# Transposing expert activations in 32x32 blocks on VectorE, with matrix columns taken in strides

## Chip, core and metric

The kernel runs on one core of a Trainium2 chip. The metric is device time in microseconds, from the first to the last instruction and the little around them; the median of several runs counts. The engines are TensorE (PE, with its weight loads PEld), VectorE (DVE), ScalarE (ACT), GpSimd (POOL) and SyncE (SP). SyncE's queue issues the transfers of the expert weights.

## What is computed

One layer of a diffusion backbone over 512 latent and 256 context tokens: attention and Fourier mixing, then a mixture of 32 experts, four to a token. The change touches the experts only. For each expert `e`, with the rows `xb` of the tokens that chose it:

```
g = minimum(xb @ w_gate[e] + b_gate[e], 7)
u = clip(xb @ w_up[e] + b_up[e], -7, 7)
act = g * sigmoid(1.702 * g) * (u + 1)
y = act @ w_down[e] + b_down[e]          # times the token's gate, added to its row
```

All three matrices are 1024 x 1024 in float32, 4 MB each, so 403 MB of expert weights are read.

## The kernel before

The first part (up to about 340 us) is attention, projections and the router. The rest is the mixture stage, in which the change lies.

**Units.** Experts are sorted by how many tokens they have, and each is a unit of a kind: heavy ("h", 128 slots, 4 experts), medium ("m", 96 slots used, 13 experts with the two that are always units 0 and 1), light ("l", 64 slots, 10 experts), tiny ("t", 32 slots, 5 experts). What doesn't fit goes to a loop at the end. From unit 2 on, units come in pairs: a heavy or medium one with a light or tiny one. There are ten medium-light pairs, four heavy-tiny pairs, and the first pair is medium-tiny. Within a pair the matrices alternate (`order`, L951 to L956): "gate" of the first, "gate" of the second, then both "up", then both "down".

**Weights.** Each matrix comes in four pieces of 1 MB (`load_piece`, L963 to L978) into a ring of eleven slots. Each piece holds two chunks `k` of 128 rows, which lie on the 128 partitions. A piece is issued by SyncE as soon as TensorE has done with the piece that lies in its slot.

**Matmuls.** `emit_mat` (L1650) runs eight steps `k` per matrix. `step_mm` (L1538) uses TensorE in column tiles: for a medium expert, twelve matmuls per step, each 32 tokens wide with 256 weight columns as the moving operand, four of them side by side in four tiles of 32 columns; for a light one two matmuls, 64 tokens wide with 512 weight columns; for a tiny one four, 32 wide with 256 columns. A heavy expert uses 128 columns and float32r with split operands. The trace records each float32 matmul as two MATMULs. The sums lie in PSUM (`ps`) in such a way that the partition tells the tile (which quarter or half of the weight columns, and which token), and not the token alone. A bias row is added first by a bfloat16 matmul (`biasP`).

**Between the matrices.** `glu_g` (L1458) and `glu_u` (L1468) do the activation: VectorE takes the sums out of PSUM into `t1` and `u1` (for light and tiny units `aTf` and `u1l`), ScalarE computes the sigmoid. `a_trans` (L1441) then transposes the activations, 128x128 at a time, on TensorE (`tr`, L268, line L270 in the trace) into PSUM bank 6 or 7, from which ScalarE copies them to `aTm` or `aTf` (`split_late` for heavy experts). They are the stationary operand of the "down" matrix. `y_out` scales the result and `scatter` (L1512) adds it to the token rows by one-hot matmuls.

**Order.** Everything in this stage stands in an order written out by the program. Work between matrices is a list of side tasks; after each step of a matrix up to two of them advance (`side_step`). `glu_u` yields a few times (2, 2, 3 or 5 steps by kind) ahead of `a_trans`, so that the transposes stand some steps into the next matrix. TensorE, VectorE and ScalarE each take their instructions in that order.

Of the kernel before, what the change touches and what calls it, by code (L numbers as in the profile page):

```python
# [31 lines left out]
AF = mybir.ActivationFunctionType  # L32
# [4 lines left out]
D = 1024  # L37
# [125 lines left out]
def dit_block(ctx: ExitStack, tc: tile.TileContext, x, c, cctx, c_ctx, w_mod, b_mod, n_ap, n_ao, n_fp, n_fo,  # L163
# [76 lines left out]
    def later(fn, outs, ins, age=1):  # L240
        if not manual:
            fn()
            return
        late.append([age, [touched(z) for z in outs], [touched(z) for z in ins], fn])
# [23 lines left out]
    def tr(o, i):  # L268
        guard([o], [i])
        pin(nc.tensor.transpose(o, i, ident))  # L270

    def act(o, i, f, **kw):
        guard([o] + ([kw["accum_out"]] if "accum_out" in kw else []), [i, kw.get("bias"), kw.get("scale")])
        return nc.scalar.activation(o, i, f, **kw)  # L274
# [976 lines left out]
        nc.gpsimd.memset(z.f, 0.0)  # L1251

    SLOTS = {"h": 128, "m": 128, "l": 64, "t": 32}

    def onehot_slots(kind, p_):
        n = SLOTS[kind]
# [28 lines left out]
    def tbank():  # L1285
        tb[0] = (tb[0] + 1) % len(tbanks)
        return tbanks[tb[0]]
# [152 lines left out]

    def a_trans(kind):  # L1441
        a = glu_tiles(kind)[1]
        for half in range(2 if kind in "hm" else 1):
            b = tbank()
            n = min(4, WIDTH[kind] // 128 - 4 * half)
            for k in range(n):
                c = (4 * half + k) * 128
                tr(ps[:, b, k * 128:k * 128 + 128], a[:, c:c + 128])
            src = ps[:, b, 0:n * 128].rearrange("p (k n) -> p k n", k=n)
            c4 = slice(4 * half, 4 * half + 4)  # L1450
            if kind == "h":
                split_late(aTh.r[:, c4], aTl.r[:, c4], src)
            else:
                z = (aTm if kind == "m" else aTf.f)[:, 4 * half:4 * half + n]
                later(lambda src=src, z=z: act(z, src, AF.Copy), [z], [src], age=0)
            yield

    def glu_g(kind, b):  # L1458
        t_, u_ = glu_tiles(kind)
# [78 lines left out]
    def step_mm(kind, mat, b, k, w, hi, lo, sel, xs):  # L1538

        first = k == 0  # L1540
        if kind == "h":
            xh, xl = xs
            if first and mat != "d":
                for h in range(2):
                    mm(ps[:, b + h], sel.to_broadcast([96, 128]), biasP.b[0:96, MAT[mat], h * 512:h * 512 + 512],
                       start=True, stop=False)
                first = False
            for st, mv, last in ((xh, hi, False), (xh, lo, False), (xl, hi, k == 7)):
                for h in range(2):
                    mm(ps[:, b + h], st.r[:, k], mv.r[:, h * 512:h * 512 + 512], start=first, stop=last)  # L1550
                first = False
        elif kind == "m":

            def unit(r, p):
                return (p, r) if p < 3 else (r, 3)

            def out_(r, p, n=1):
                return ps[32 * p:32 * p + 32, b + r // 2, 256 * (r % 2):256 * (r % 2) + 256 * n]


            both = ps[96:128, b].rearrange("p (r n) -> p r n", r=2)
            if first:
                bias = biasP.b[0:96, MAT.get(mat, 0)]
                if mat != "d":
                    for p in range(3):
                        mm(out_(0, p, 2), sel.to_broadcast([96, 32]), bias[:, 0:512], start=True, stop=False)
                else:
                    sel = selb.b[0:96, NS + 2:NS + 3]
                mm(both, sel.to_broadcast([96, 32]), bias[:, None, 768:D].to_broadcast([96, 2, 256]), start=True,
                   stop=False)  # L1570
                if mat != "d":
                    for p in range(4):
                        q = unit(2, p)[1]
                        mm(out_(2, p), sel.to_broadcast([96, 32]), bias[:, q * 256:q * 256 + 256], start=True, stop=False)
            for r in range(3):
                for p in range(4):
                    g, q = unit(r, p)
                    n = 1
                    if mat != "d":
                        st = xs[:, k, 32 * g:32 * g + 32]  # L1580
                    else:
                        fq, c = k // 2, k % 2
                        st = xs[:, 2 * fq + c, 32 * g:32 * g + 32] if fq < 3 else xs[:, 2 * g + c, 96:128]
                        if first and p < 3 and r < 2:
                            if r:
                                continue
                            n = 2
                    mm(out_(r, p, n), st, w[:, q * 256:q * 256 + 256 * n],
                       start=first and mat == "d" and (p < 3 or r == 2), stop=k == 7 and r > 0)
        else:  # L1590
            v, n = (64, 512) if kind == "l" else (32, 256)
            a, c = k // (n // 128), k % (n // 128)
            st = xs[:, c, v * a:v * a + v]
            if first and mat != "d":
                for h in range(128 // v):
                    mm(ps[v * h:v * h + v, b, 0:n], sel.to_broadcast([96, v]),
                       biasP.b[0:96, MAT[mat], h * n:h * n + n], start=True, stop=False)
                first = False
            for h in range(128 // v):
                mm(ps[v * h:v * h + v, b, 0:n], st, w[:, h * n:h * n + n], start=first, stop=k == 7)  # L1600

    def sel_of(u):
        kind, e, r = units[u]
# [69 lines left out]
    for i, (u, m) in enumerate(order):  # L1673
        kind = kinds[u]
        if i:
            pu, was = order[i - 1]
            pk, pb = kinds[pu], bank[pu, was]
            if was == "g":
                add(glu_g(pk, pb), True)
            elif was == "u":  # L1680
                acted[pu] = add(chain(glu_u(pk, pb, {"h": 2, "m": 2, "l": 3, "t": 5}[kind]), a_trans(pk)), True)
            else:
                finish(summed)
                y_out(pu, pk, pb)
                if pu == 1:
                    summed = add(chain(chain_back(pu), scatter(pu)))
                elif pk in "lt":
                    summed = add(chain(chain_back(pu - 1), chain_back(pu), scatter(pu - 1, pu)))
        if i == 5:
            summed = add(chain(bdown(), chain_back(0), scatter(0)))  # L1690
        if i == 1:
            ready[1] = add(x_of(1))
        elif i == 2:
            add(fetch_of(2))
            add(fetch_of(0))
            add(fetch_of(3))
        elif i == 3:
            ready[2] = add(chain(x_of(2), fetch_of(4)))
            add(chunk_plan())
        elif i == 6:  # L1700
            ready[3] = add(chain(x_of(3), fetch_of(5)))
        elif m == "d" and u >= 2 and u + 2 < NU:
            x_ = x_of(u + 2)
            ready[u + 2] = add(chain(x_, fetch_of(u + 4)) if u + 4 < NU else x_)
        if (u, m) == (NU - 4, "g"):
            ntot, jcnt = W(1, dt=I32), W(1)
            cp(ntot.i, incl.f[:, NE - 1:NE])
            V.memset(jcnt.f, 0.0)
            n_over = nc.values_load(ntot.i[0:1, 0:1], min_val=0, max_val=48, skip_runtime_bounds_check_because=SKIP)
        if m == "g":  # L1710
            finish(ready.get(u))
        elif m == "d":
            finish(acted.get(u))
        if i + 1 == len(order):
            break
        emit_mat(i)
        if i == 0:
            settle()
            t1, u1 = W(D), W(D)
            xT1 = W(8, 128)  # L1720
        elif i == 1:
            while side:
                finish(side.pop(0))
            queued.close()
            free(lg, mask, maskb, Ub, onesb)
            aTh, aTl = R(8, 128), R(8, 128)
            aTm = alias(aTh, 6, 128)
            yh, yl = R(D), R(D)
            acc = [W(D) for _ in range(4)]

            bdr = acc[3]
            for r in range(3):
                nc.sync.dma_start(bdr.f[32 * r:32 * r + 32], b_d)
        elif i == 4:
            settle()
            free(xT1)
            bd, gT, g3 = R(D), R(512), W(4, 96)
            xTf = W(4, 128)
        elif i == 6:
            while side and side[0] is not ready[3]:  # L1740
                finish(side.pop(0))
            settle()
            free(bd, g3, gT)
            aTf, u1l, yz = W(4, 128), W(512), R(D)

    while side:
        finish(side.pop(0))
# [136 lines left out]
```

## Time and profile before

| | us |
|---|---|
| three runs | 1412.1, 1416.8, 1417.2 |
| median | 1416.8 |
| the profiled execution, its own time | 1413.2 |
| its span | 1411.4 |
| TensorE busy | 1345.5 |
| VectorE busy | 719.9 |
| ScalarE busy | 409.3 |
| stage from 360 to 1380: TensorE's granted clock | 1.00, but for one stretch |

[...] In rows in order of time, the first column is the start and the second how long the group was busy; a group ends where the next begins or a little after, since matmuls overlap. "128*32 128x256" is a stationary operand of 128 rows and 32 columns with a moving one of 128 rows and 256 columns. A row takes the shape of its first instruction, so that one that begins with a bias matmul (96 rows, bf16) may hold others. Matmul ends are modelled; starts are measured.

### The profile page before, as it was taken

To read this page: it belongs to the slowest core of one execution; us is meant where nothing else is said; L and a number is where in the kernel's file an instruction comes from. 1 tells how busy PE (TensorE), PEld (TensorE's weight loads), DVE (VectorE), ACT (ScalarE), POOL (GpSimd) and SP (SyncE) were. 2 spreads that over 40 slices of the span, in tenths; PEclk is the share of its full clock that TensorE was granted. 3 is DMA by queue.
4 is the path that set the end of the run, shared out by engine and by line. 5 is a ranking of instruction groups with operands and counts; after the bars stand their busy time and mean duration, and the time that the engine had idled before them with its cause. 6 is when DMAs were issued, how large, how long until landed. Compare 5 with 4: busy or idle time off the path is not lost. (4 is left out here: it accounts for less than half of the span.)

```text
span 1411.4 us, 30490 instructions
## 1 busy us (share of the span) xinstructions
PE 1345.5 (95%) x12966; PEld 798.2 (57%) x12967; DVE 719.9 (51%) x1329; ACT 409.3 (29%) x634; POOL 121.8 (9%) x90
## 2 busy tenths in 40 slices
PE   5998999998999999999999999999999999999993
PEld 3766887877554545466444454654544466444572
DVE  4676777755452424268423335762324287232575
ACT  5565455632110101035110103421111154010352
POOL 4355000013000000000000000000000000000002
PEclk8999999999998999999999999999999999999997
DMA  9865003667887999999999999999999999999993
GB/s 343 306 229 189 1 0 106 216 228 313 315 295 298 408 397 408 379 409 392 405 409 379 409 374 409 396 408 406 393 384 385 401 395 408 402 408 375 408 380 122
DMA packets 126496, 468.86 MB, mean 332 GB/s; under 512 B 10976, under 2 KB 12316, under 8 KB 126356
## 3 DMA queue, kind: packets, MB, share of 16 engines
q1 hardware_dynamic: 121540, 454.44, 83.2%
q0 software_dynamic: 4816, 12.43, 2.3%
q8 instruction: 103, 1.69, 0.5%
q14 instruction: 37, 0.30, 0.1%
HBM read 464.05 MB, written 6.31 MB: 333 GB/s over the span
## 5 line engine op out<-in xcount | busy, mean ns | idle before, releaser
L266 PE MATMUL ps<-s,s 128*32 128x256 f32 (+11 forms) x5364 | 892.4, 417 | 28.7 <-DMA s<-in_w_mod_dram 8.4
L266 PEld LDWEIGHTS ps<-s,s 128*128 128x128 f32 (+4 forms) x5033 | 510.8, 155 | 315.2 <-issue 182.2
L266 PE MATMUL ps<-s,a 128*32 128x256 f32 (+1 forms) x7026 | 412.7, 383 | 0.0
L266 PEld LDWEIGHTS ps<-s,a 128*32 128x32 f32 x7026 | 216.7, 110 | 158.5 <-issue 18.9
L274 ACT ACTIVATE s<-s 128x1024 fp32r<-128x1024 f32 (+8 forms) x196 | 175.9, 927 | 361.7 <-DVE s L283 308.4
L278 DVE TENSOR_TENSOR s<-s,s 128x1024 fp32r<-128x1024 f32 (+11 forms) x316 | 208.4, 686 | 32.3 <-ACT s L274 28.6
L274 ACT ACTIVATE s<-ps 128x512 fp32r<-128x512 f32 (+5 forms) x168 | 91.3, 553 | 246.0 <-PE ps L266 127.1
L278 DVE TENSOR_TENSOR s<-s,ps 128x512 f32<-128x512 f32 (+1 forms) x129 | 86.5, 682 | 82.1 <-PE ps L266 81.7
L285 DVE TENSOR_SCALAR s<-ps 128x768 f32<-128x768 f32 (+3 forms) x32 | 26.3, 823 | 185.1 <-PE ps L266 185.1
L270 PE MATMUL ps<-s,s 128*128 128x128 f32 x575 | 96.6, 288 | 15.3 <-DVE s L283 9.9
L1302 POOL DMA_INDIRECT s<-hx_d,s x31 | 32.4, 1045 | 893.3 <-PE ps L266 613.2
L270 PEld LDWEIGHTS ps<-s,s 128*128 128x128 f32 x575 | 66.4, 143 | 73.7 <-issue 45.8
L293 DVE COPY s<-ps 128x4 f32<-128x4 f32 (+5 forms) x66 | 23.7, 359 | 141.0 <-PE ps L266 117.0
L274 ACT ACTIVATE a<-ps 128x512 f32<-128x512 f32 (+1 forms) x48 | 25.9, 540 | 219.0 <-PE ps L270 219.0
L278 POOL TENSOR_TENSOR s<-s,s 128x1024 f32<-128x1024 f32 (+1 forms) x23 | 53.7, 2339 | 272.9 <-DVE s L278 211.4
L289 DVE SCALAR_TENSOR_TENSOR s<-ps,s,s 32x256 fp32r<-32x256 f32 (+5 forms) x64 | 46.2, 721 | 58.0 <-ACT s L274 52.0
L274 ACT ACTIVATE s<-ps,s 32x256 fp32r<-32x256 f32 (+7 forms) x68 | 44.8, 669 | 97.9 <-PE ps L266 90.5
L297 DVE TENSOR_TENSOR s<-ps,s 128x512 fp32r<-128x512 f32 (+1 forms) x92 | 60.6, 667 | 22.9 <-ACT s L274 22.8
L283 DVE TENSOR_SCALAR s<-ps 128x768 f32<-128x768 f32 (+4 forms) x33 | 26.5, 803 | 77.6 <-PE ps L266 77.5
L274 ACT ACTIVATE s<-s,s 128x1 f32<-128x1 f32 (+4 forms) x70 | 43.2, 644 | 13.8 <-DVE s L289 7.7
L297 DVE TENSOR_TENSOR s<-s,s 128x192 fp32r<-128x192 f32 (+5 forms) x32 | 36.0, 1144 | 8.5 <-ACT s L274 8.5
L289 DVE SCALAR_TENSOR_TENSOR s<-s,s,s 128x512 fp32r<-128x512 f32 (+5 forms) x48 | 36.8, 796 | 5.9 <-ACT s L274 4.6
(77 smaller groups left out, 289.4 us busy)
## 6 DMA issues: line engine op xcount, KB each, us to landing
s<-in_w_gate_dram SPq DMA_DIRECT2D x128, 1024.0 KB, 10.9
s<-in_w_up_dram SPq DMA_DIRECT2D x128, 1024.0 KB, 10.8
s<-in_w_down_dram SPq DMA_DIRECT2D x128, 1024.0 KB, 7.9
s<-in_w_mod_dram SPq DMA_DIRECT2D x32, 512.0 KB, 4.6
s<-in_w_mod_dram SPq DMA_DIRECT2D x8, 1024.0 KB, 16.3
s<-in_x_dram SPq DMA_DIRECT2D x8, 512.0 KB, 8.3
s<-in_w_out_dram SPq DMA_DIRECT2D x8, 512.0 KB, 5.1
s<-in_w_in_dram SPq DMA_DIRECT2D x1, 2560.0 KB
```

What stands on the lines that cost most here:

```text
L266: pin(nc.tensor.matmul(o, a, b, start=start, stop=stop))
L270: pin(nc.tensor.transpose(o, i, ident))
L274: return nc.scalar.activation(o, i, f, **kw)
L278: return eng.tensor_tensor(o, a, b, op=op)
L283: eng.tensor_scalar(o, a, s1, s2, op0=op0)
L285: eng.tensor_scalar(o, a, s1, s2, op0=op0, op1=op1)
L289: V.scalar_tensor_tensor(o, a, s, b, op0=op0, op1=op1)
L293: eng.tensor_copy(o, i)
L297: later(lambda: eng.tensor_tensor(lo, src, hi, op=OP.subtract), [lo], [src, hi])
L1302: nc.gpsimd.indirect_dma_start(out=xg[kind], out_offset=None, in_=src, in_offset=bass.IndirectOffsetOnAxis(ap=idxs.i[:, u:u + 1], axis=0), ...
```

## The change

Medium, light and tiny activations are no longer transposed by TensorE. VectorE does it, in blocks of 32x32: one instruction takes 128 partitions by eight blocks of 32 columns and turns each block over within its 32 partitions. A medium unit needs three such instructions, a light one two, a tiny one one. `glu_u` no longer yields ahead of them, so they stand right behind the activation. The heavy units keep their transposes.

For the result to be a full transpose, the sums of "gate" and "up" have to lie differently in PSUM: partition 32q + i must hold token i and those columns whose number modulo 128 lies in the q-th 32. So in these two matrices each column tile q now takes its 256 moving columns in eight runs of 32, 128 apart (`cols`), and the bias likewise. Medium and tiny units keep their number of matmuls; light ones go from two 64-wide of 512 columns to eight 32-wide of 256. The "down" matrix keeps its form for each kind and only reads the stationary operand from its new place (`aTm` and `aTf` have new shapes of the same size).

```diff
+    ROWS = {"h": 128, "m": 96, "l": 64, "t": 32}
...
     def a_trans(kind):
         a = glu_tiles(kind)[1]
-        for half in range(2 if kind in "hm" else 1):
-            b = tbank()
-            n = min(4, WIDTH[kind] // 128 - 4 * half)
-            for k in range(n):
-                c = (4 * half + k) * 128
-                tr(ps[:, b, k * 128:k * 128 + 128], a[:, c:c + 128])
-            src = ps[:, b, 0:n * 128].rearrange("p (k n) -> p k n", k=n)
-            c4 = slice(4 * half, 4 * half + 4)
-            if kind == "h":
+        if kind == "h":
+            for half in range(2):
...
                 split_late(aTh.r[:, c4], aTl.r[:, c4], src)
-            else:
-                z = (aTm if kind == "m" else aTf.f)[:, 4 * half:4 * half + n]
-                later(lambda src=src, z=z: act(z, src, AF.Copy), [z], [src], age=0)
-            yield
+                yield
+            return
+        for s in range(ROWS[kind] // 32):
+            o = (aTm if kind == "m" else aTf.f)[:, :, 32 * s:32 * s + 32]
+            i_ = a[:, 256 * s:256 * s + 256].rearrange("p (b r) -> p b r", r=32)
+            guard([o], [i_])
+            V.transpose(o, i_)
+        yield
...
+        elif mat != "d":
+
+            n = ROWS[kind] // 32
+
+            def x_cols(o):
+                m, v = {"m": (8, 0), "l": (4, 64), "t": (2, 32)}[kind]
+                return xs[:, k % m, v * (k // m) + o:v * (k // m) + o + 32]
+
+            def cols(z, q):
+                return z.rearrange("p (b q r) -> p q b r", q=4, r=32)[:, q]
+
+            def tile_(q, s, n=1):
+                return ps[32 * q:32 * q + 32, b + s // 2, 256 * (s % 2):256 * (s % 2) + 256 * n]
+
+            if first:
+                for s in range(0, n, 2):
+                    m = min(2, n - s)
+                    for q in range(4):
+                        z = cols(biasP.b[0:96, MAT[mat]], q)
+                        o = tile_(q, s, m)
+                        if m == 2:
+                            o = o.rearrange("p (m b r) -> p m b r", m=2, r=32)
+                            z = z[:, None].to_broadcast([96, 2, 8, 32])
+                        mm(o, sel.to_broadcast([96, 32]), z, start=True, stop=False)
+            for s in range(n):
+                for q in range(4):
+                    mm(tile_(q, s), x_cols(32 * s), cols(w, q), start=False,
+                       stop=k == 7 and (s % 2 == 1 or s + 1 == n))
...
-                acted[pu] = add(chain(glu_u(pk, pb, {"h": 2, "m": 2, "l": 3, "t": 5}[kind]), a_trans(pk)), True)
+                acted[pu] = add(chain(glu_u(pk, pb, {"h": 2, "m": 2, "l": 3, "t": 5}[kind] if pk == "h" else 0), a_trans(pk)), True)
...
-            aTm = alias(aTh, 6, 128)
+            aTm = alias(aTh, 8, 96)
...
-            aTf, u1l, yz = W(4, 128), W(512), R(D)
+            aTf, u1l, yz = W(8, 64), W(512), R(D)
```

What this does to the order of the instructions is seen best on TensorE in a light unit's "up" matrix (first medium-light pair). Here `s_67` is the identity, `s_2877` is `u1` with the medium unit's activations, `s_3463` (then `s_3458`) the light unit's tokens, and the other names are ring slots with weights. Before:

```order
L266 MATMUL ps<-s_2343,s_3463 64x512 x4
L266 MATMUL ps<-s_2537,s_3463 64x512 x4
L270 MATMUL ps<-s_67,s_2877 128x128 x4
L266 MATMUL ps<-s_2545,s_3463 64x512 x2
L270 MATMUL ps<-s_67,s_2877 128x128 x2
L266 MATMUL ps<-s_2545,s_3463 64x512 x2
L266 MATMUL ps<-s_2553,s_3463 64x512 x4
```

And now:

```order
L266 LDWEIGHTS s_2597
L266 MATMUL ps<-s_1972,s_2597 32x512
L266 MATMUL ps<-s_2343,s_3458 32x256 x16
L266 MATMUL ps<-s_2537,s_3458 32x256 x16
L266 MATMUL ps<-s_2545,s_3458 32x256 x16
L266 MATMUL ps<-s_2553,s_3458 32x256 x16
```

The two groups of transposes are gone, nothing stands in their places, and every 64x512 matmul has become four of 32x256.

On VectorE at the same place, from the medium unit's activation to the place table of a later unit (`s_2876` and `s_2877` are `t1` and `u1`, `s_3747` and `s_3748`, now `s_3737` and `s_3738`, are `aTf` and `u1l`). Before:

```order
L285 TENSOR_SCALAR s_2877<-ps 128x768
L289 SCALAR_TENSOR_TENSOR s_2877<-s_2877,s_2876 128x768
L285 TENSOR_SCALAR s_3748<-ps 128x512
L289 SCALAR_TENSOR_TENSOR s_3748<-s_3748,s_3747 128x512
L278 TENSOR_TENSOR s_2724<-s_2335,s_2732 128x128
```

And now (`a_3014` is `aTm`):

```order
L285 TENSOR_SCALAR s_2877<-ps 128x768
L289 SCALAR_TENSOR_TENSOR s_2877<-s_2877,s_2876 128x768
L1459 STREAM_TRANSPOSE a_3014<-s_2877 128x8x32 x3
L285 TENSOR_SCALAR s_3738<-ps 128x512
L289 SCALAR_TENSOR_TENSOR s_3738<-s_3738,s_3737 128x512
L1459 STREAM_TRANSPOSE s_3737<-s_3738 128x8x32 x2
L278 TENSOR_TENSOR s_2724<-s_2335,s_2732 128x128
```

Five instructions have come in, each group right behind the activation it transposes.

The third place is VectorE in a heavy "down" matrix, where it splits the heavy unit's weights into two parts (the 128x1024 rows) a few steps ahead of TensorE. Before:

```order
L285 TENSOR_SCALAR s_3748<-ps 128x256
L289 SCALAR_TENSOR_TENSOR s_3748<-s_3748,s_3747 128x256
L278 TENSOR_TENSOR s_2594<-s_2695,s_2593 128x1024
L278 TENSOR_TENSOR s_2588<-s_2708,s_2587 128x1024
L278 TENSOR_TENSOR s_2724<-s_2335,s_2732 128x128
```

And now:

```order
L285 TENSOR_SCALAR s_3738<-ps 128x256
L289 SCALAR_TENSOR_TENSOR s_3738<-s_3738,s_3737 128x256
L1459 STREAM_TRANSPOSE s_3737<-s_3738 128x8x32
L278 TENSOR_TENSOR s_2594<-s_2695,s_2593 128x1024
L278 TENSOR_TENSOR s_2588<-s_2708,s_2587 128x1024
L278 TENSOR_TENSOR s_2724<-s_2335,s_2732 128x128
```

One transpose has come in ahead of the splits. The orders of GpSimd and of SyncE have no new and no missing instruction.

## Rows read from the trace of the kernel before

**Rows 1.** Stretches: busy us by engine, clock granted, DMA share, rate.

```profile
core 0: us, PE busy (x) PEld busy (x) DVE busy (x) ACT busy (x) POOL busy (x), PEclk, DMA share, GB/s
...
600.00:800.00 200.00, 197.83 (x1993) 106.27 (x1995) 95.45 (x174) 48.45 (x67) 6.44 (x6) 1.00 1.01 400
...
433.60:447.20 13.60, 12.87 (x60) 6.20 (x64) 6.08 (x10) 0.00 (x0) 0.00 (x0) 0.50 0.51 194
```

**Rows 2.** Waits from 360 to 1380 us: total, times, longest.

```profile
...
PEld ps L266 <- DVE s L278: 20.4, 25, 2.2
PEld ps L266 <- DMA s<-in_w_up_dram: 2.9, 10, 0.4
...
SPq L978 <- PE ps L266: 672.7, 315, 8.4
```

**Rows 3.** DMA, 600 to 1380 us: rate by slice, total, an issue group.

```profile
GB/s 408 379 410 407 410 402 408 409 355 410 408 355 399 408 409 384 409 408 403 408 408 353 393 408 399 363 409 408 386 409 407 395 411 407 395 360 408 409 383 371
DMA packets 81003, 309.49 MB, mean 397 GB/s; under 512 B 5639, under 2 KB 5643, under 8 KB 80924
...
s<-in_w_up_dram SPq DMA_DIRECT2D x96, 1024.0 KB, 10.8
```

**Rows 4.** TensorE in order of time: a light "gate", then that expert's "up".

```profile
696.85 7.27 PE L266 MATMUL ps<-s,s 96*64 96x512 bf16 x34
...
714.85 3.84 PE L266 MATMUL ps<-s,s 96*64 96x512 bf16 x18
718.63 0.66 PE L270 MATMUL ps<-s,s 128*128 128x128 f32 x4
...
720.59 2.79 PE L266 MATMUL ps<-s,s 128*64 128x512 f32 x12
```

**Rows 5.** TensorE in order of time: a medium "up", then that expert's "down".

```profile
704.28 0.28 PE L266 MATMUL ps<-s,s 96*32 96x256 bf16 x4
...
704.39 10.54 PE L266 MATMUL ps<-s,a 128*32 128x256 f32 x192
...
723.32 1.68 PE L266 MATMUL ps<-s,a 128*32 128x512 f32 x18
724.93 0.66 PE L270 MATMUL ps<-s,s 128*128 128x128 f32 x4
725.52 1.50 PE L266 MATMUL ps<-s,a 128*32 128x256 f32 x24
726.95 0.66 PE L270 MATMUL ps<-s,s 128*128 128x128 f32 x4
```

**Rows 6.** TensorE in order of time: inside a heavy "down" matrix.

```profile
660.06 0.60 PE L270 MATMUL ps<-s,s 128*128 128x128 f32 x4
660.41 1.64 PE L266 MATMUL ps<-s,s 128*128 128x512 f32 x6
661.89 0.38 PE L270 MATMUL ps<-s,s 128*128 128x128 f32 x2
662.03 2.36 PE L266 MATMUL ps<-s,s 128*128 128x512 f32 x9
```

**Rows 7.** VectorE in order of time: under the same heavy "down" matrix.

```profile
659.58 0.41 DVE L285 TENSOR_SCALAR s<-ps 128x256 f32<-128x256 f32 x1
...
660.37 2.55 DVE L278 TENSOR_TENSOR s<-s,s 128x1024 fp32r<-128x1024 f32 x3
```

**Rows 8.** Groups by line and shape, 360 to 1400 us: busy us, mean ns.

```profile
L285 DVE TENSOR_SCALAR s<-ps 128x768 f32<-128x768 f32 x13 | 12.5, 958 | 107.8 <-PE ps L266 107.8
...
L285 DVE TENSOR_SCALAR s<-ps 128x256 f32<-128x256 f32 x5 | 2.1, 415 | 2.8 <-PE ps L266 2.8
...
L274 ACT ACTIVATE a<-ps 128x512 f32<-128x512 f32 x35 | 20.9, 598 | 208.5 <-PE ps L270 208.5
```

**Rows 9.** Matmuls of two short stretches: ns min/median/max; value projection first.

```profile
L266 PE MATMUL ps<-s,s x19: 277/281/287, 111.2 to 113.4; 128*128 128x256 f32 x19
...
L266 PE MATMUL ps<-s,s x12: 280/282/392, 147.6 to 149.0; 128*128 128x256 f32 x11, 128*128 128x512 f32 x1
```

More of the change, by code (lines that the diff above doesn't have):

```diff
@@ L1442, in a_trans @@
         a = glu_tiles(kind)[1]
-        for half in range(2 if kind in "hm" else 1):
-            b = tbank()
-            n = min(4, WIDTH[kind] // 128 - 4 * half)
-            for k in range(n):
-                c = (4 * half + k) * 128
-                tr(ps[:, b, k * 128:k * 128 + 128], a[:, c:c + 128])
-            src = ps[:, b, 0:n * 128].rearrange("p (k n) -> p k n", k=n)
-            c4 = slice(4 * half, 4 * half + 4)
-            if kind == "h":
-                split_late(aTh.r[:, c4], aTl.r[:, c4], src)
-            else:
-                z = (aTm if kind == "m" else aTf.f)[:, 4 * half:4 * half + n]
-                later(lambda src=src, z=z: act(z, src, AF.Copy), [z], [src], age=0)
-            yield
+        if kind == "h":
+            for half in range(2):
+                b = tbank()
+                for k in range(4):
+                    c = (4 * half + k) * 128
+                    tr(ps[:, b, k * 128:k * 128 + 128], a[:, c:c + 128])
+                src = ps[:, b].rearrange("p (k n) -> p k n", k=4)
+                c4 = slice(4 * half, 4 * half + 4)
+                split_late(aTh.r[:, c4], aTl.r[:, c4], src)
+                yield
[6 more added lines that the diff above has]
+        yield
     def glu_g(kind, b):
@@ L1558, in out_ @@
                 return ps[32 * p:32 * p + 32, b + r // 2, 256 * (r % 2):256 * (r % 2) + 256 * n]
-            both = ps[96:128, b].rearrange("p (r n) -> p r n", r=2)
             if first:
[L1563 to L1574, printed above, removed]
+                both = ps[96:128, b].rearrange("p (r n) -> p r n", r=2)
+                zero = selb.b[0:96, NS + 2:NS + 3].to_broadcast([96, 32])
+                mm(both, zero, biasP.b[0:96, 0][:, None, 768:D].to_broadcast([96, 2, 256]), start=True, stop=False)
             for r in range(3):
@@ L1578, in step_mm @@
                     n = 1
[L1579 to L1589, printed above, removed]
+                    if first and p < 3 and r < 2:
+                        if r:
+                            continue
+                        n = 2
+                    mm(out_(r, p, n), xs[:, k, 32 * g:32 * g + 32], w[:, q * 256:q * 256 + 256 * n],
+                       start=first and (p < 3 or r == 2), stop=k == 7 and r > 0)
         else:
             v, n = (64, 512) if kind == "l" else (32, 256)
[L1592 to L1598, printed above, removed]
             for h in range(128 // v):
-                mm(ps[v * h:v * h + v, b, 0:n], st, w[:, h * n:h * n + n], start=first, stop=k == 7)
+                mm(ps[v * h:v * h + v, b, 0:n], xs[:, k, 0:v], w[:, h * n:h * n + n], start=first, stop=k == 7)
     def sel_of(u):
```

## The prediction

> **What bounds the kernel now.** I read the stretches first, then the waits, the DMA view, and last the row order of TensorE inside one pair of experts. From 600 to 800 us TensorE is busy for 197.8 of 200 us at full clock, and DMA is busy all the time too [rows 1]. Two engines at 100% leave it open which one sets the pace. The waits decide it: in the whole mixture stage TensorE's weight loads waited 2.9 us for expert weights from DMA, while SyncE's queue, which issues those transfers, waited 672.7 us for TensorE to release a ring slot [rows 2]. So the weights lie ready and TensorE is the path. DMA is close behind: its slices stand at 407 to 411 GB/s and dip to 353 to 400 where the ring is full, mean 397 [rows 3]. The room until DMA itself is the bound is 1 - 397/409 = 2.9% of those 780 us, about 23 us. A microsecond taken off TensorE between 360 and 1380 us should therefore come off the end, up to that room.
>
> **The change, part by part.** The sum is made against the profiled execution, 1413.2 us (span 1411.4).
>
> *Transposes that leave TensorE.* There are 13 medium experts (six transposes each, in a group of four and one of two), ten light (one group of four) and five tiny (one group of two): 128 transposes. Their price is not their busy time but by how much the matrix around them grows.
> - Ten medium experts have theirs inside the light expert's "up" matrix. A light "gate" matrix without them takes 7.27 us; the "up" matrix with both groups runs from 714.85 to 720.59 + 2.79 = 723.38, so 8.53 [rows 4]. Difference 1.26, times ten: 12.6 us.
> - Ten light experts have theirs in the next medium "down" matrix. Two groups of four start 2.02 us apart with 24 matmul records between them, and 24 records undisturbed take 10.54/8 = 1.32 [rows 5]: 0.70 each, 7.0 us.
> - Units 0, 1 and 2 have theirs between 32-column matmuls. The four cost 0.70; the two cost 0.49, which is less by two transposes of 0.105 (the difference between 0.35 for four and 0.14 for two in [rows 6], halved). That is 1.2 for units 0 and 2 each, and 1.0 for unit 1, where a scatter follows that has to change the column width anyway: 3.4 us. The tiny expert of the first pair: 0.5.
> - Four tiny experts have theirs inside a heavy "down" matrix, among 128-column matmuls, from 661.89 to 662.03 [rows 6]: 0.14 each, 0.6 us.
>
> Together 24.1 us.
>
> *Changes of column width.* The same four transposes cost 0.35 among 128-column matmuls (660.06 to 660.41 [rows 6]) and 0.70 among 32-column ones, so going to another width and back costs 0.35, at most 0.17 per change. Seen alone, from 64 to 32 columns: the "down" matrix starts 0.06 before the light matrix ends at 723.38, while within 32 columns the next matmuls start 0.17 before the end of the ones ahead (704.39 against 704.28 + 0.28) [rows 4, 5]. That is 0.11. The light "gate" and "up" matrices go from 64 to 32 columns, so four changes per medium-light pair vanish: 40 x 0.11 = 4.4 us, bounds 0 and 40 x 0.17 = 6.8.
>
> *The first two matrices.* The number of columns streamed stays. A light step was two 64-wide matmuls of 512 columns and is eight 32-wide ones of 256. The old matrix takes 7.27 with its two bias matmuls [rows 4], 32 records in about 7.0; 128 records of the new form at 10.54/192 = 0.055 [rows 5] make 7.0. Nothing, both ways. What no row shows is a moving operand of 32-element runs, 128 elements apart, in four column tiles at once. The nearest is the attention's value projection, whose moving operand is two runs of 128 elements with a gap of 128: 281 ns per matmul of 256 columns, against 282 where the 256 columns are contiguous [rows 9]. I take zero. A gain has no reason, since the same columns pass; the loss has no row above it and is a rival below.
>
> *Transposes that VectorE gets.* 13 x 3 + 10 x 2 + 5 = 64 instructions of 128x256. No row shows one. The nearest is a 128x256 tensor_scalar, 0.415 us; the far bound is 0.958, three times the columns [rows 8], the lower one nothing. I take 0.42. [...] What hides them is the matrix in between. A medium expert's chain after its "up" is 0.96 + 0.96 + 3 x 0.42 = 3.2 us, under a light "up" of over 7; a light one's is shorter and lies under a medium "down" of over 10. In the first pair the cover is only a tiny "up", 64 records x 0.055 = 3.5 us: still enough, but at 0.958 it is short by 1.3 once. Queued behind them on VectorE are the next expert's place tables, whose matmuls stand some steps further down TensorE's row. Only in the four heavy-tiny pairs is there no cover: around 660 us VectorE's operations follow one another without a gap while it splits heavy weights [rows 7], and TensorE waits for such splits (20.4 us in 25 times [rows 2]). I charge 4 x 0.42 = 1.7 us (bounds 0 and 3.8).
>
> *Copies that leave ScalarE.* 41 evacuations, 0.60 us for one of 128x512 [rows 8]. ScalarE stood waiting for TensorE before them, so nothing is gained on the path. POOL and SyncE keep their order; the transfers start earlier because slots come free earlier.
>
> Sum: 24.1 + 4.4 - 1.7 = 26.8 us, so 1386.4 against the profiled execution. The median shown, 1416.8, lies 3.6 above that one, which by itself would give 1390. I put the forecast between, **1388 us**. What moves it within the case: no gain from column widths and the dear VectorE bound, 7.8 up; the dear width change and free transposes, 4.1 down; and the half clock from 433.6 to 447.2 [rows 1], which may fall away or lengthen when the work ahead of it ends 2 us sooner, up to 6.8 either way. They won't all fall together: 1379 to 1398.
>
> **Rivals.**
>
> *DMA takes over.* Of the saving, eight medium-light pairs lie between 600 and 1380 us: 8 x (1.26 + 0.70 + 0.44) = 19 us, of 23 us of room. Against it: an "up" piece lands 10.8 us after its issue in the median [rows 3], so with eleven slots and 1024 KB every 2.6 us some seven pieces are landed or in use. For it: 83% of the room is used up, and 2.9% is only as good as the plateau. If half of these 19 us were lost, 1398; if all, 1407. Chance 9%, time 1400.
>
> *Slower: the strided moving operand.* The "gate" and "up" matrices of medium, light and tiny experts are 26 x 48 + 20 x 32 + 10 x 16 = 2048 rounds of four overlapping matmuls, each of 10.54/48 = 0.22 us [rows 5]. Each nanosecond per round is 2 us. The change turns into a loss from 26.8/2048 = 13 ns, 6% of a round. With 10% (22 ns) the time is 1388 + 45 = 1433. For it: every column tile jumps every 32 elements, and no row has that. Against it: the gap within the value projection costs nothing [rows 9]. Chance 9%.
>
> *Four times as many instructions.* Light "gate" and "up" go from 32 to 128 records; if TensorE needed a fixed time to issue each, they would grow. Medium matrices show 55 ns per record [rows 5], so such a floor lies at or below that; were it an eighth above, 20 x 128 records x 7 ns would add 18 us: 1406. Chance 2%. [...]
>
> *Nothing happens on TensorE.* If the time of the transposes stayed as waits, the gain would be under 5 us. The changed order has nothing in their places, and no row shows what TensorE would wait for there. Chance 1%; 1410.
>
> **How the numbers follow.** The forecast has 79%, DMA 9, stride 9, instructions 2, nothing 1. The forecast's own range holds most of its 79%; to reach eight in ten I take in the nearer half of the DMA case: 1378 to 1403. 0.5%, about what a measurement of this kernel can tell from no change, is 7 us. Faster: the forecast, nearly all of DMA and the instructions, 0.88. Same: small stride costs and nothing, 0.04. Slower: the rest of the stride case, 0.08.
>
> **What would show it.** Right: a light "up" takes as long as its "gate", about 7.2 us; a medium "down" keeps only the two groups of four that transpose a later expert's input; TensorE's weight loads still wait for DMA by a few us in all; DMA's mean from 600 us on rises from 397 to about 406 GB/s; VectorE has 64 transposes near 0.42 us. Wrong in the stride: a medium "up" of 192 records longer than 10.5 us, a round above 0.22. Wrong in DMA: TensorE waits for weights, and the slices stand at 409 without dips. Wrong in the chain: TensorE waits for VectorE's transposes at the start of a "down" matrix, in the first pair above all.

## The result and the profile after

The changed kernel takes 1389.4 us (median of four runs, 1387.3 to 1391.6) against 1414.5 for the kernel before, run beside it: ratio 0.983, 95% interval 0.981 to 0.985, so 25 us less. The forecast was 1388, range 1378 to 1403. The profiled execution took 1389.0 (span 1387.2), 24.2 less than the profiled one of before.

The stretch from 600 to 800 us and the DMA view from 600 to 1360 us, after (columns as in [rows 1] and [rows 3]):

```profile
600.00:800.00 200.00, 197.21 (x2348) 114.25 (x2348) 102.76 (x195) 46.97 (x64) 8.00 (x8) 1.00 1.03 408
```

```profile
GB/s 409 408 408 409 408 407 408 407 404 408 408 399 407 409 408 408 409 407 406 409 407 401 409 408 395 409 407 409 408 408 409 402 409 406 395 410 408 409 410 320
DMA packets 80471, 307.51 MB, mean 405 GB/s; under 512 B 5624, under 2 KB 5628, under 8 KB 80382
...
s<-in_w_up_dram SPq DMA_DIRECT2D x96, 1024.0 KB, 12.7
s<-in_w_down_dram SPq DMA_DIRECT2D x96, 1024.0 KB, 15.3
s<-in_w_gate_dram SPq DMA_DIRECT2D x90, 1024.0 KB, 18.0
```

TensorE is still busy all the time, but the dips to 353 to 400 GB/s of [rows 3] are almost gone: of 23 us of room little is left. An "up" piece now lands 12.7 us after its issue, where it was 10.8.

TensorE in order of time, the same medium-light pair as in [rows 4, 5]: light "gate", medium "up", light "up", then the start of the medium "down":

```profile
687.19 7.64 PE L266 MATMUL ps<-s,s 96*32 96x512 bf16 x140
694.65 10.54 PE L266 MATMUL ps<-s,a 128*32 128x256 f32 x192
705.01 7.31 PE L266 MATMUL ps<-s,s 96*32 96x512 bf16 x132
...
713.76 0.66 PE L270 MATMUL ps<-s,s 128*128 128x128 f32 x4
714.35 1.50 PE L266 MATMUL ps<-s,a 128*32 128x256 f32 x24
715.78 0.65 PE L270 MATMUL ps<-s,s 128*128 128x128 f32 x4
716.37 6.68 PE L266 MATMUL ps<-s,a 128*32 128x256 f32 x120
```

The light "up" has no transposes and takes as long as its "gate": from bias to bias 7.15 and 7.13 us (the first row also holds the eight bias records of the next matrix). The medium "up" takes 10.54 us for 192 records with strided columns, to the last digit what it took before [rows 5]: here the stride costs nothing. Two groups of transposes are left in the medium "down"; they turn a later expert's tokens.

The new instructions, and the waits from 360 to 1380 us (us in total, times, longest):

```profile
L1459 DVE STREAM_TRANSPOSE a<-s x39: 401/404/447, 362.3 to 1278.6; 128x256 f32<-128x256 f32 x39
L1459 DVE STREAM_TRANSPOSE s<-s x25: 400/445/447, 458.1 to 1347.0; 128x256 f32<-128x256 f32 x25
```

```profile
PEld ps L266 <- DVE s L278: 24.8, 28, 2.3
ACT s L274 <- DMA s<-in_w_down_dram: 13.9, 4, 8.3
PE ps L266 <- DVE s L278: 10.0, 12, 1.8
PEld ps L266 <- ACT s L274: 2.8, 5, 0.9
PEld ps L266 <- DMA s<-in_w_up_dram: 2.4, 7, 0.4
PEld ps L266 <- DMA s<-in_w_gate_dram: 1.3, 4, 0.4
```

A transpose takes 0.40 to 0.45 us. TensorE itself still waits for weights by a few us only (3.7 in these two rows; 2.9 for "up" before [rows 2]). But ScalarE, which makes the first part of the split of heavy weights, waits 13.9 us for "down" weights; there is no such row before.

**The ledger.** I laid the starts of all matrices (their bias matmuls) of the two traces side by side. How much later (+) or earlier (-) each part ended:

```
before the mixture stage (to 336 us, code not changed)      -2.15
units 0 and 1: -1.23 and -0.36                              -1.6
clock between 430 and 485 us (0.88 in both, see the end)     0.0
first pair: medium transposes -1.22, tiny ones -0.45        -1.7
ten medium-light pairs, -2.35 each (66.16 us -> 63.81)      -23.3
  light "up" -1.31, medium "down" -0.73, column widths -0.30
  (the sum is 0.2 short of ten times 2.35 at the borders to other pairs)
four heavy-tiny pairs, +0.44 each (as in the first two)     +1.8
third heavy pair, on top                                    +0.8
fourth heavy pair and the end, on top                       +2.0
total                                                       -24.2
```

### The profile page after: what moved, and what is told of

The parts are those of the page before. It is cut to its first block, busy times and chain, and to the rows that moved or that the text cites. A ratio compares the mean times of both kernels' runs of the same rounds, so it can differ in the third digit from the quotient of the medians.

```text
span 1387.2 us, 34148 instructions
## 1 busy us (share of the span) xinstructions
PE 1316.4 (95%) x14798; PEld 831.8 (60%) x14799; DVE 743.3 (54%) x1393; ACT 389.2 (28%) x593; POOL 121.9 (9%) x90
## 5 line engine op out<-in xcount | busy, mean ns | idle before, releaser
L266 PE MATMUL ps<-s,s 128*32 128x256 f32 (+7 forms) x7324 | 882.1, 387 | 32.4 <-DVE s L278 10.0
L266 PEld LDWEIGHTS ps<-s,s 128*32 128x32 f32 (+3 forms) x6953 | 547.5, 140 | 301.6 <-issue 108.2
L266 PEld LDWEIGHTS ps<-s,a 128*32 128x32 f32 x7026 | 223.8, 110 | 157.4 <-issue 17.9
L274 ACT ACTIVATE s<-ps 128x512 fp32r<-128x512 f32 (+5 forms) x153 | 83.6, 555 | 284.2 <-PE ps L270 143.0
L270 PE MATMUL ps<-s,s 128*128 128x128 f32 (+1 forms) x447 | 74.2, 289 | 16.4 <-DVE s L283 10.2
L270 PEld LDWEIGHTS ps<-s,s 128*128 128x128 f32 (+1 forms) x447 | 53.3, 145 | 51.3 <-issue 14.9
L274 ACT ACTIVATE a<-ps 128x512 f32<-128x512 f32 x22 | 13.2, 598 | 145.2 <-PE ps L270 145.1
```

The source lines that it names most:

```text
L266: pin(nc.tensor.matmul(o, a, b, start=start, stop=stop))
```

## Experiments

Each timed against the kernel before in the same session (1410.5 to 1410.9 us there), and read by the same ledger.

**Is there room in DMA, and how much?** Two kernels leave out the TensorE transposes of the experts' tokens, in the kernel before and in the changed one:

```diff
+    u_all = False
...
-                tr(ps[:, b, k * 128:k * 128 + 128], xg[kind][:, c:c + 128])
+                if u_all:
+                    tr(ps[:, b, k * 128:k * 128 + 128], xg[kind][:, c:c + 128])
```

> The kernel before, with the TensorE transposes of the experts' tokens left out (some 40 groups of two or four; ScalarE still copies whatever lies in PSUM, so the tokens of the experts are wrong). By the rows of the changed kernel such a group costs 0.70 us among 32-column matmuls and up to 0.89 among 64-column ones, in all about 28 us. Theory T (TensorE alone sets the end, in both kernels): 1414 - 28 = 1386 us. Theory D (the changed kernel is at the limit of its weight transfers; the kernel before has room of about 23 us): about 1390, most of the 28 comes off.

> The changed kernel, with the same token transposes left out on TensorE. Theory T: 1389 - 28 = 1361 us, and TensorE's and the split's waits for weights stay at a few us. Theory D: weights are transferred at 405 GB/s in the mean from 600 to 1360 us where the plateau is 409, so there is about 1%, 8 or 9 us, left: about 1380, and the rest of the 28 us turns up as waits for weights.

Measured: 1388.7 us in the kernel before (ratio 0.983, 0.980 to 0.986), so 22 of the estimated 28 came off. Even there the room is used up: DMA's mean from 600 to 1340 us is 406 GB/s, and ScalarE waits 7.6 us for "down" weights, in three places. In the changed kernel 1384.8 (against 1387.6 and 1389.4 for that kernel itself): 3 to 5 of 28, less than the 8 or 9 that theory D left. Its waits from 360 to 1380 us:

```profile
PEld ps L266 <- DVE s L278: 40.2, 45, 3.0
PE ps L266 <- DVE s L278: 16.5, 18, 2.5
ACT s L274 <- DMA s<-in_w_down_dram: 16.2, 2, 8.1
PEld ps L266 <- ACT s L274: 11.9, 9, 2.4
PEld ps L266 <- DMA s<-in_w_down_dram: 9.3, 12, 1.5
```

Beside the same rows of the changed kernel (24.8, 10.0, 13.9 and 2.8; the last had 0.4): what TensorE no longer does, it waits. Theory D holds against theory T: with the change the program stands within a few us of what its weight transfers allow.

**One half alone.** Only the medium experts changed, then only light and tiny ones (`a_trans`, `step_mm` and the yields of `glu_u` ask for the kind):

```diff
+    NEW = "m"          # the other kernel: "lt"
...
-        elif mat != "d":
+        elif mat != "d" and kind in NEW:
```

> Only the 13 medium experts get the strided columns and VectorE transposes; light and tiny ones as in the kernel before. By the ledger of the changed kernel: 10 x 1.26 in the light 'up' matrices (the column widths stay as they were, so the 0.35 per pair for them does not come) and 2.8 in units 0 to 2, so 15.4 off: 1399 us. Theory T and theory D agree on the time; D adds that the sixteen shares of a weight piece land within 3 us of each other as in the kernel before, and that no heavy pair waits for weights, since DMA still has pauses. If the gain of the light 'up' came from its narrower matmuls instead of the transposes, this kernel gains under 8.

> Only light and tiny experts get them; medium ones keep their TensorE transposes. By the ledger: 10 x (0.73 in the medium 'down' matrix + 0.35 for four column widths that no longer change) + 0.45 in the first pair - 4 x 0.44 in the heavy pairs, so 9.5 off: 1405 us. With m_only the two add up to 24.9, by theory T what the full change gains; by theory D the full change gains about 2.8 less than the sum, the waits of its third and fourth heavy pair, and neither part alone has these waits.

Measured: 1394.3 us (0.989, 0.987 to 0.990), 16.2 off for 15.4 expected; and 1401.4 (0.994, 0.993 to 0.996), 9.2 off for 9.5. In the ledgers the first has -1.25 in every one of the ten light "up" matrices and 0.00 elsewhere in the pairs; the second -0.73 in every medium "down", four times -0.08 to -0.11 at the changes of column width, and +0.43 to +0.45 in heavy pairs. Neither has a wait of ScalarE for weights, though in the second VectorE's transposes stand in the heavy pairs as in the full change. The sum of the two, 25.4, is within the scatter of the full change; that 2.7 us are lost together shows only in the traces.

**What the heavy pairs wait for.** The trace records when each of the sixteen shares of a transfer lands. From the first to the last share of a piece, median us:

```
80 us from       480   640   800   960  1120  1280
before           1.9   1.9   2.1   1.6   1.9   2.2
changed          2.4   4.3   5.5   8.4   9.7  10.4
one piece less   2.2   2.3   1.8   2.4   2.0   2.2
```

These are the pieces whose sixteen shares all stand in the trace, few of them in the first two kernels; a second execution of the changed kernel, with records of most pieces, gives 2.6, 4.1, 5.7, 8.9, 9.3 and 10.7. In the changed kernel the shares drift apart. A few shares lag, and not the whole: in that second execution, from 1120 to 1200 us, the first share lands 8.5 us after its issue (7.9 from 480 us on), the thirteenth 13.0, the last 18.3. The third line is this kernel:

```diff
+        if kind == "l" and m == "g" and h == 0:
+            return
         nc.sync.dma_start(slot.f, src.rearrange("e (k p) f -> p (e k) f", p=128)[:, 2 * h:2 * h + 2])
```

> The changed kernel, with the first of the four weight pieces of every light 'gate' matrix not transferred (the matrix uses what lies in that ring slot, so light experts are wrong): 10 of 384 pieces, one per medium-light pair, 26 us of DMA's time; no instruction of TensorE, VectorE or ScalarE changes. Theory D (in the changed kernel the sixteen shares of a piece drift apart, from 2.4 us at 500 us to 10.4 at 1280, because DMA never pauses, and the heavy pairs, whose weights must be there early for the split, wait for the last share): the spread stays under about 4 us, the third heavy pair loses its 0.8 us and the last one its 2.0 us of waiting, so about 2.8 off: 1386.5 us. Rival V (these waits come from the VectorE transposes that stand ahead of the splits): the waits stay, 1389.

Measured: 1382.4 us (0.980, 0.978 to 0.982), 5 to 7 below the changed kernel, where 2.8 were expected. No compute instruction differs. By the ledger what was lost comes back: 0.77 in the third heavy pair, 0.24 and 2.2 in the last one and the end (0.5 of it behind the last matmul). Another 6.2 of the 9.0 us by which its profiled execution is shorter are the clock's, between 426 and 498 us (granted from 420 to 460 us: 0.87 in the changed kernel, 1.00 here). The last pair is the firm part: its 2.0 us stand in both executions of the changed kernel, and 1.8 in the kernel with runs of four further down. The third pair lost 0.77 in one execution, 0.46 in the other and nothing in that kernel, so that its 0.8 are no fixed price. The last heavy pair on ScalarE and then TensorE, first in the changed kernel:

```profile
1331.06 1.06 ACT L274 ACTIVATE s<-s 128x1024 fp32r<-128x1024 f32 x1 [0.28 <-PE ps L266]
1340.38 1.06 ACT L274 ACTIVATE s<-s 128x1024 fp32r<-128x1024 f32 x1 [8.25 <-DMA s<-in_w_down_dram]
```

```profile
1342.11 5.43 PE L266 MATMUL ps<-s,s 128*128 128x512 f32 x20 [0.41 <-ACT s L274]
1348.59 14.32 PE L266 MATMUL ps<-s,s 128*128 128x512 f32 x107 [1.05 <-DVE s L278]
```

and with one piece less per pair:

```profile
1324.35 1.06 ACT L274 ACTIVATE s<-s 128x1024 fp32r<-128x1024 f32 x1 [0.28 <-PE ps L266]
1325.73 1.06 ACT L274 ACTIVATE s<-s 128x1024 fp32r<-128x1024 f32 x1 [0.32 <-PE ps L266]
1333.30 0.60 ACT L274 ACTIVATE s<-ps 128x512 fp32r<-128x512 f32 x1 [6.51 <-PE ps L270]
```

```profile
1334.35 5.49 PE L266 MATMUL ps<-s,s 128*32 128x256 f32 x28
1340.27 14.22 PE L266 MATMUL ps<-s,s 128*128 128x512 f32 x107 [0.43 <-DVE s L278]
```

The split at 1340.38 waited 8.25 us for its weights and held up the splits behind it. Of the sixteen shares of its piece thirteen had landed by 1333.37, the others landed at 1337.40, 1339.81 and 1340.22; the split started 0.16 us after the last. With the pauses (DMA's mean from 600 to 1360 us is 390 GB/s, slices go down to 346) it stands right behind the one before, at 1325.73, and what is left of TensorE's wait is 0.43, about what a transpose costs in the first two heavy pairs (0.44). So the weights that came late, not VectorE, cost the last pair its 2.0 us. That the lag of a few shares made them late is read from the traces, no run changes it by itself: with the pauses both the lag and the load are gone. Which shares lag, and why those, the trace doesn't show.

**VectorE in the heavy pairs, and under the others.** The tiny experts back on TensorE (`NEW = "ml"`), and every VectorE transpose issued twice:

> The changed kernel with the five tiny experts as in the kernel before (transposes on TensorE, columns not strided); medium and light ones as changed. Every heavy-tiny pair took 0.44 us longer after the change, so if VectorE's transpose ahead of the heavy splits is the cause, 0.44 comes off in each of the four and 0.45 comes back in the first pair: 1.3 off, 1388 us, and no more. If the 0.44 are something else (the narrower light pair ahead, code), the pairs stay as long as with the full change and the time is 1389.5 to 1390. The waits for weights in the third and fourth heavy pair stay by theory D or grow by the same 0.44.

```diff
             V.transpose(o, i_)
+            V.transpose(o, i_)
```

> The changed kernel with every one of the 64 VectorE transposes issued twice, 27 us more of VectorE. If the matrices in between cover them as the prediction says, medium-light pairs stay at 63.8 us to a tenth, and only the heavy pairs grow, by 0.42 us each, so +1.7: 1391 us. If the cover in the medium-light pairs were thin, TensorE would wait at the start of the 'down' matrices: up to 10 x 5 x 0.42 = 21 more, 1410.

The first took 1389.0 us (0.983, 0.982 to 0.985): no change to be seen. Its ledger gives -0.43 and -0.46 in the first two heavy pairs and +0.45 in the first pair, as expected, but +0.2 and +0.3 in the third and fourth, where the weights were not there any sooner (ScalarE waits 8.2 us for "down" weights, once): the last pair keeps its loss without any VectorE transpose in it. The second took 1393.9 (0.986, 0.982 to 0.990). All ten medium-light pairs kept their time to 0.01 us: the cover there is ample. The first two heavy pairs grew by 0.50; the last two, bound by weights (ScalarE waits 10.5 us for "down" ones), didn't. In unit 1 it lost 3.1 us: 1.44 are a longer wait (the rows below), and 1.7 are the 48 records behind it, at 4.48 us instead of 2.80. The granted clock from 400 to 408 us was 0.79 there, and 1.00 at this place in the changed kernel. In the first pair it lost 1.8. Of these 0.8 are a stretch at the half clock that the changed kernel has too (granted 0.57 from 476 to 480 us), just behind the pair's border, and that comes back there. The other 1.0 is a new wait, in steps too short for the list of waits: VectorE's doubled transposes end at 462.11 and, the last, at 462.91, and TensorE's records of the medium "down" go on at 462.13 and 462.97 (VectorE, then TensorE):

```profile
462.46 0.45 DVE L1460 STREAM_TRANSPOSE a<-s 128x256 f32<-128x256 f32 x1
```

```profile
462.13 2.32 PE L266 MATMUL ps<-s,a 128*32 128x512 f32 x17
```

From the first record of that matrix to the next group of TensorE transposes it takes 2.68 us, and 1.62 in the changed kernel. So the cover in the first pair, the tiny "up", was enough for three transposes and was not for six. At unit 1, VectorE (changed kernel) and TensorE (changed kernel, then doubled):

```profile
398.15 1.10 DVE L1459 STREAM_TRANSPOSE a<-s 128x256 f32<-128x256 f32 x3
399.17 0.32 DVE L293 COPY s<-s 128x384 f32<-128x384 f32 x1
```

```profile
399.54 0.64 PE L270 MATMUL ps<-s,s 128*96 128x128 f32 x4 [0.53 <-DVE s L293]
```

```profile
401.66 0.64 PE L270 MATMUL ps<-s,s 128*96 128x128 f32 x4 [1.97 <-DVE s L293]
```

Queued behind the three transposes is the copy of the gates (`g3` in `bdown`), and TensorE stands waiting to transpose it. So at unit 1 the change made a new wait, 0.53 us.

**How short may the runs be?** Runs of 4 elements, and single ones, instead of 32 in `cols`:

```diff
-                return z.rearrange("p (b q r) -> p q b r", q=4, r=32)[:, q]
+                return z.rearrange("p (b q r) -> p q b r", q=4, r=4)[:, q]     # one kernel
+                return z.rearrange("p (b r q) -> p q b r", q=4, r=32)[:, q]    # the other
```

> The changed kernel, but each column tile takes every fourth column (256 single elements, 16 bytes apart) instead of eight runs of 32, so the columns of the result stand in another order and it is not the layer's output. The changed kernel's rounds of four matmuls take 0.22 us with runs of 32, as with contiguous columns. If TensorE reads a moving operand of float32 at any stride at the same pace, 1389 us; if the stride begins to cost as the runs get short, each 0.01 us per round adds 20 us over 2048 rounds: 1409 and more.

> The changed kernel with each column tile taking its 256 columns in 64 runs of four (16 bytes each, 64 apart; the columns of the result stand in another order and it is not the layer's output). Single elements 16 bytes apart doubled a round of four matmuls, from 0.22 to 0.46 us; runs of 32 cost nothing. If what counts is how many 16-byte pieces of the weights are touched per column, runs of four are free: 1389 us and rounds of 0.22. If it is the length of a run as such (a fixed cost per run), runs of four lie between: a round of 0.28 us and more, over 1500 us.

Single elements 16 bytes apart: 1878 us (1.330, 1.328 to 1.332). Runs of four: 1389.2, from one run. A medium "up", first with runs of four, then single:

```profile
695.31 10.54 PE L266 MATMUL ps<-s,a 128*32 128x256 f32 x192
```

```profile
701.36 22.23 PE L266 MATMUL ps<-s,a 128*32 128x256 f32 x192
```

The rival of the strided operand is real, but far off: 16 contiguous bytes were enough (10.54 us, 0.22 per round), single elements doubled the matrix (22.23). Why they do, no run shows.

**Two tries for a faster version.** Tiny experts on TensorE with the heavy pairs one pair earlier, and the heavy weights split two steps ahead instead of three; the changed kernel again beside them:

```diff
-HEAVY_AT = (3, 7, 11, 14)
+HEAVY_AT = (2, 6, 10, 13)
...
-    NB, LA = 4, 3
+    NB, LA = 4, 2          # the second kernel
```

> The changed kernel itself once more, to stand beside the two versions that follow: 1389 us.

> The changed kernel with the tiny experts back on TensorE, and the heavy-tiny pairs one pair earlier (third, seventh, eleventh and fourteenth instead of fourth, eighth, twelfth and fifteenth), so that the program ends with a medium-light pair, which needs no split of weights ahead of TensorE. Theory D: the waits in the last heavy pair come from weights that land late, and a medium-light pair, which asks for a weight only when TensorE reaches it, does not have them: 2 off for the end, up to 1 for the tiny experts: 1386.5 us. If what was waited for at the end only turns up in the last medium-light pair (the last weights land at the same time in any order), 1389.

> The changed kernel with the heavy weights split two steps ahead of TensorE instead of three. Theory D: the weights are then needed one step (1.7 us) later, so the waits of the third and fourth heavy pair (0.8 and 2.0 us) shrink to about 0.3, 2.5 off: 1387 us. But the split chain (ScalarE 1.06 us, VectorE 1.22 us, queued behind other work) has one step less of cover: where VectorE's transpose and activation stand ahead of it, TensorE may wait up to 1.7 us in each of the eight heavy matrices: up to 1400.

Measured: 1387.6 for the changed kernel, 1386.9 for the first (0.984, 0.982 to 0.985; no difference that the runs can tell, though its profiled execution is 2.5 us shorter), 1390.0 for the second (0.986, 0.984 to 0.988). In the first ScalarE still waits 13.7 us for "down" weights, and TensorE stands 2.6 us ahead of the fourth heavy pair: the waits moved. In the second ScalarE has no wait for weights left, as expected (the third pair's loss is missing in the kernel with runs of four too), but TensorE waits longer for the split: +1.9 in each of the first two heavy pairs. That was the second case told ahead. Neither is measurably faster than the change.

## Why the prediction was right

- *What bounds the kernel.* Right for the kernel before: an estimated 28 us off TensorE gave 22. The room of about 23 us was about right too: after the change only 3 to 5 more came off.
- *Transposes that leave TensorE.* 1.26 per light "up": -1.25 in the half that changes it alone. 0.70 per medium "down": -0.73. Units 0 and 2: 1.2 forecast, 1.23 and 1.22 measured. Unit 1: 1.0 forecast, 0.36 measured. There the step on what is queued behind the transposes on VectorE, "the next expert's place tables, whose matmuls stand some steps further down TensorE's row", was incomplete: at unit 1 the copy of the gates stands there, and TensorE waits for it (0.53 us).
- *Column widths.* 0.44 per pair forecast; measured 0.36 to 0.39, that is 0.08 to 0.11 per change.
- *Strided columns, number of records.* Nothing forecast, nothing measured. The time of 1406 for four times the records takes a floor an eighth above 55 ns; no run shows it: a medium "up" takes 10.54 us for 192 records as before, 55 ns each, and a light "gate" of 128 records 7.15 us, where the one of 32 took 7.27.
- *VectorE.* 0.42 us per transpose, right (0.40 to 0.45). The cover in medium-light pairs is ample, right. The first pair's is thin, as said: three transposes fit under its 3.5 us, six did not. 0.42 in each heavy pair without cover: right in size, though net of the 0.14 of the transposes removed there a heavy pair should have grown by 0.28, and it grew by 0.44.
- *DMA.* The step that failed, small as it was. I weighed the room as a mean over 780 us and asked whether TensorE would wait. The saving all but fitted into the mean, but 2.7 us in this execution (2.0 of them firm) were given back in another way: without pauses the shares of a piece drifted apart (2.4 us from 480 us on, 10.4 from 1280 on), and ScalarE and VectorE, which split heavy weights ahead of TensorE, need them earlier than TensorE does.
- *The sum.* 26.8 forecast within the stage. By the ledger the stage gained 24.8 (1.6 + 1.7 + 23.3 - 1.8), and DMA took 2.7 back: 22. Another 2.15 of the profile's 24.2 lie ahead of the stage, where nothing changed, and differ from run to run (the granted clock from 85 to 130 us was 0.92 before, and 1.00 and 0.96 in the two executions of the changed kernel). The median's 25 and the ledger's 22 lie within the interval of the ratio (21 to 27 us); that the forecast of 1388 came so close to the median is in part luck.

## What to carry to other kernels

When TensorE sets the pace and transfers are close behind, as here, price an instruction by how much the matrix around it grows, and take from the sum no more than the transfers have left; past that, what TensorE saved here it waited (3 to 5 us came off, of an estimated 28). Ask of the room not only TensorE but every engine that reads a transfer earlier than it (here ScalarE, which waited 13.9 us). In this kernel the work moved to another engine cost nothing under a long matrix (ten medium-light pairs kept their time to 0.01 us with twice the transposes), about its whole time where that engine already worked without gaps (0.44 us in a heavy pair), and a wait where something small that TensorE needs was queued behind it (0.53 us at unit 1).

## What was not expected of the hardware

- With DMA at 405 to 408 GB/s without a pause, the sixteen shares of a 1 MB transfer drifted from 2.4 to over 10 us apart in 800 us, because a few of them fell behind (of the piece that landed at 1340.22 the last three shares took 4.0 to 6.9 us longer than the thirteenth). With one piece less per medium-light pair, by an estimate from 1 MB at 405 GB/s 2.6 us of every 64, they stayed at 1.8 to 2.4.
- A moving float32 operand in runs of 16 bytes, 64 apart, streams as fast as a contiguous one (10.54 us per 192 records); single elements 16 bytes apart take 22.23.
- The same 72 records of the first scatter took 13.73, 12.56 and 8.01 us, in the kernel before and in two executions of the same changed kernel. The mean granted clock from 420 to 460 us was 0.83, 0.87 and 1.00, and TensorE had been idle ahead of them in all three (2.5 to 2.9 us):

```profile
434.33 13.73 PE L266 MATMUL ps<-s,s 96*128 96x512 f32 x72 [2.87 <-DVE s L283]
```

```profile
430.58 12.56 PE L266 MATMUL ps<-s,s 96*128 96x512 f32 x72 [2.87 <-DVE s L283]
```

```profile
431.40 8.01 PE L266 MATMUL ps<-s,s 96*128 96x512 f32 x72 [2.47 <-DVE s L283]
```

In the first execution of the changed kernel the granted clock was 0.50 from 432 to 442.2 us, as in the second stretch of [rows 1]. So up to 6 us between two executions (13.73 and 8.01) are the half clock's, and belong to no edit; in the ledgers this stretch is set apart.
